# Two matmuls without a use beside each step of the triangular inversion in layer 1

## The chip, the cores and the metric

The kernel runs on one core of a Trainium2 chip. The metric is the device time of one execution in microseconds (us). Before the change it was 2228.44 us, the median of three runs (2225.9 to 2229.92).

A core has five engines, each with a queue of its own that it works through in order: TensorE (PE in the profile; its weight loads are shown apart as PEld), VectorE (DVE), ScalarE (ACT), GpSimd (POOL) and SyncE (SP), which only issues transfers here. An instruction that has to wait for another engine holds up everything behind it in its own queue.

## The reference

Two layers of a transformer trunk over 512 latent tokens and 256 context tokens of width 1024, in fp32. What matters here is the mixer: one input projection feeds a gated DeltaNet in chunks of 64 tokens and a latent attention, side by side. The DeltaNet solves a unit triangular system for every chunk, head and direction.

```python
for l in range(DEPTH):                                   # DEPTH = 2
    h  = modulate(rmsnorm(x, norm1_g[l]), sh1, sc1)
    hc = modulate(rmsnorm(ctx, norm1_g[l]), sh1c, sc1c)
    y, yc = hybrid_mixer(h, hc, ...)                     # input projection, DeltaNet and attention, output projection
    x = x + g1 * y
    x = x + g2 * swiglu(modulate(rmsnorm(x, norm2_g[l]), sh2, sc2), w_gate[l], w_up[l], w_down[l])
    if not last:                                         # the context's own output is only needed in layer 0
        ctx = ctx + g1c * yc
        ctx = ctx + g2c * swiglu(modulate(rmsnorm(ctx, norm2_g[l]), sh2c, sc2c), ...)
return rmsnorm(x, final_norm_g)

# within gdn_chunked, for each chunk of 64 tokens:
a_mat = jnp.where(strict, jnp.einsum('bhnid,bhnjd->bhnij', kb, k) * decay, 0.0)
sol = lax.linalg.triangular_solve(a_mat + eye, rhs, left_side=True, lower=True)
u, w = sol[..., :DV], sol[..., DV:]                      # used by the scan over the chunks
```

## The kernel before

Activations lie with the features on the 128 partitions and the tokens along the row. A matrix product in fp32 is made of three products in fp32r: weights and activations are split into a high and a low part (ScalarE copies the high part, VectorE subtracts it for the low one, `load_w` and `split`), and `gemm` (line 222) issues high x high, high x low and low x high into one PSUM bank. A matmul of line 222 on the latent tokens has a 128 x 128 weight tile and 512 columns.

The program is written as eleven generators, one for each piece of a layer, most of them run once for each layer: the context's input projection, chain, attention and FFN, and the latent stream's `lat_in` (input projection), `lat_chain` (DeltaNet), `mla_prep` and `mla_att` (attention) and `lat_ffn` (output projection and FFN). `weave` runs them by turns, by ranks and paces in the table `TUNE`, and a scheduler behind it settles the order of each engine's queue. Layer 1's context pieces (`ctx_in1`, and `ctx_chain` with l = 1) are woven into layer 0's `lat_ffn`.

`gdn_pre` prepares a group of DeltaNet heads. It is called for the context (CTX, all four head pairs at once) and for the latent stream's head pairs 0 and 1 (X01) and 2 and 3 (X23) one after the other, in each layer: six calls. In the middle of each call the 32 x 32 diagonal blocks are inverted by forward substitution, all blocks side by side:

```python
for r in range(31):
    n, m = 31 - r, r + 1
    t3 = tmp[:, 0:n * m].rearrange("p (a b) -> p a b", b=m)
    tt(t3, L3[:, r + 1:32, r:r + 1].to_broadcast([P, n, m]), M3[:, r:r + 1, 0:m].to_broadcast([P, n, m]))
    tt(M3[:, r + 1:32, 0:m], M3[:, r + 1:32, 0:m], t3, SUB)
    yield 1, 0, 0.5
```

Each step is two VectorE operations (`tt`, recorded at line 140) on up to 256 elements a row. Behind the 31 steps TensorE multiplies the inverted blocks together (lines 586 and 587, then 596 and 597), two multiply-adds on VectorE complete the inverse, and the products of line 621 apply it. `gdn_scan` (its first matmuls at lines 668, 680 and 691) then runs over the chunks.

Other lines that the text names: `together` (233) issues matmuls that share a bank on different parts of the array, among them the modulation of layer 1 (four of 32 x 512 for each tile of weights; its transposition is line 304); `rms_rows` (336) sums squares over the features with a matmul by ones, in fp32, which the hardware runs in pieces; `prep` in the attention finds an upper bound of the scores by matmuls and VectorE's reductions (932 and 933 for latent keys, 937 and 938 for context keys, 945 turns the result); `attend` makes the scores (960), and 977 is the reciprocal of its sums. ScalarE's operations by `act` are at line 152, and VectorE's multiply-add `stt` at 149. PSUM has eight banks, of which the tag "C" has two.

Of the kernel before, what the change touches and what calls it, by code (L numbers as in the profile page):

```python
# [20 lines left out]
P = 128  # L21
# [85 lines left out]
def trunk_kernel(ctx, tc, xin, cc, wmod, small, win, wuq, wuk, wuv, wout, wgu, wdn, cst, rope, out):  # L107
    nc = tc.nc
    V, A, G, PE = nc.vector, nc.scalar, nc.gpsimd, nc.tensor
# [14 lines left out]
    def nm(s):  # L124
        uid[0] += 1
        return f"{s}_{uid[0]}"

    def slot(tag, dt=F32, w=None):
        width = WIDTH[tag]
        t = sp.tile([P, width], dt, name=nm(tag), tag=tag, bufs=BUFS[tag])  # L130
        return t[:, 0:w or width]

    def ps(tag):
        return pp.tile([P, 512], F32, name=nm("ps" + tag), tag=tag, bufs=PSB[tag])
# [4 lines left out]
    def tt(out, a, b, op=ALU.mult, e=None):  # L139
        (e or V).tensor_tensor(out=out, in0=a, in1=b, op=op)  # L140
# [34 lines left out]
    ident_r = cp.tile([P, P], F32R, name="ident_r")  # L175
# [49 lines left out]
    def gemm_f32(w, xs, o):  # L225
        for k, x_ in enumerate(xs):
            PE.matmul(o, w[:, k * P:k * P + P], x_, start=k == 0, stop=k == len(xs) - 1)  # L227

    def together(mms):
        prev = None  # L230
        for mm in mms[::-1]:
            with nullcontext() if prev is None else tc.issue_after(prev.ins):
                prev = mm()  # L233
# [220 lines left out]
    def gdn_pre(l, st, hjs, kf, qf, vf, gt, res):  # L454
# [112 lines left out]
        V.transpose(out=L3, in_=bd.rearrange("p (u i) -> p i u", i=32))  # L567
        M3 = M.rearrange("p (i j) -> p i j", j=32)
        tmp = slot("st", w=256)
        for r in range(31):  # L570
            n, m = 31 - r, r + 1
            t3 = tmp[:, 0:n * m].rearrange("p (a b) -> p a b", b=m)
            tt(t3, L3[:, r + 1:32, r:r + 1].to_broadcast([P, n, m]), M3[:, r:r + 1, 0:m].to_broadcast([P, n, m]))
            tt(M3[:, r + 1:32, 0:m], M3[:, r + 1:32, 0:m], t3, SUB)
            yield 1, 0, 0.5
        x1, x2 = bd, L
        V.transpose(out=x1.rearrange("p (u r) -> p r u", r=32), in_=M3)
# [33 lines left out]
        for dst, lh, rh in ((us, vv, (vs, vs)), (W, ke, vv)):  # L611
            for a in range(0, U, 4):
                pt = ps("B")
                pv = pt.rearrange("p (n d i) -> p n d i", d=2, i=64)
                for q in range(4):
                    n, hi = divmod(a + q, nh)
# [441 lines left out]
    class Mix:  # L1058
# [55 lines left out]
        def stage(self, g):  # L1114
            f = self.f[g]
            if g in self.spilled:
                for kind in "kqv":
                    t = slot("g4")
                    nc.sync.dma_start(out=t.rearrange("p (j t) -> p j t", j=len(g)), in_=f[kind].rearrange("j p t -> p j t"))
                    f[kind] = t  # L1120
            return gdn_pre(self.l, self.st, g, f["k"], f.get("q"), f["v"], self.gates, self.pre[g])
# [329 lines left out]
```

## Time and the profile before

| | |
|---|---|
| median of three runs | 2228.44 us |
| the profiled execution | 2224.78 us |
| its span in the trace | 2223.0 us |
| TensorE busy | 2032.2 us (91%), 16048 matmuls |
| VectorE busy | 1474.6 us (66%), 2904 instructions |
| ScalarE busy | 889.5 us (40%), 1583 instructions |
| mean granted clock of TensorE | 0.946 |

The span is the time from the first to the last instruction that the trace shows of one execution. A busy share is a mean over the whole program and says nothing of a single stage. The granted clock is given as a share of 2.4 GHz: TensorE runs at 2.4 or at 1.2 GHz, and a number between 0.50 and 1.00 is a mixture over the stretch.

### The profile page before, as it was taken

Reading aid. Unit: us, or ns where it says so; the run is one execution under the profiler, and the core shown is the slowest. Engines: PE = TensorE matmul, PEld = TensorE weight load, DVE = VectorE, ACT = ScalarE, POOL = GpSimd, SP = SyncE. Lnnn points to the kernel's source line nnn. Section 1 sums busy time; section 2 is a strip of 40 time slices with the busy share of each in tenths; the row PEclk is TensorE's granted clock in tenths of the full one; section 3 lists DMA queues with packets and bytes.
Section 4 is the critical chain, followed back from the end, with each engine's and each line's share of the span. In section 5 each row is a group of like instructions: output and inputs, shape, how many; then the busy total and the mean of one; then the engine's idle time right before and its main releaser. Section 6 shows DMA issues by size and latency. Waiting matters only on the chain.

```text
span 2223.0 us, 40501 instructions
## 1 busy us (share of the span) xinstructions
PE 2032.2 (91%) x16048; PEld 1591.7 (72%) x16048; DVE 1474.6 (66%) x2904; ACT 889.5 (40%) x1583; POOL 69.6 (3%) x249
## 2 busy tenths in 40 slices
PE   5999988889998899899999998987976989999996
PEld 2876777789995557778888885765644677888885
DVE  4688668876689767769444457887687555444445
ACT  4445365444443534552323234534422234222233
POOL 0000001000000000000000000000000000000000
PEclk8999998899999999999999999996986999999998
DMA  8345514344446202242222236621110022233332
GB/s 327 136 155 188 172 32 124 112 143 132 127 155 208 85 11 80 93 146 91 86 76 96 89 113 221 190 78 29 44 34 11 30 76 76 95 99 96 96 99 76
DMA packets 130638, 240.48 MB, mean 108 GB/s; under 512 B 15185, under 2 KB 30065, under 8 KB 130449
## 3 DMA queue, kind: packets, MB, share of 16 engines
q1 hardware_dynamic: 124592, 224.16, 31.1%
q0 software_dynamic: 5856, 13.74, 2.3%
q8 instruction: 126, 2.06, 0.4%
q14 instruction: 64, 0.52, 0.1%
HBM read 228.30 MB, written 6.91 MB: 106 GB/s over the span
## 4 chain that ended last, share of the span: by engine, by line
PE 76%; DVE 10%; DMA 6%; ACT 5%; issue 3%; SPq 0%; POOL 0%; ACTq 0%; DVEq 0%; POOLq 0%
PE psA L222 35%; PE psM L222 14%; PE psF L222 4%; PE psB L960 3%; PE psA L233 2%; PE psA L227 2%; PE psB L621 2%; PE psM L233 2%; PE psC L668 1%; DVE fl L140 1%; DMA m<-wmod 1%; ACT t L152 1%; DVE g L140 1%; PE psC L680 1%; PE psC L691 1%
## 5 line engine op out<-in xcount | busy, mean ns | idle before, releaser
L222 PE MATMUL psA<-hx,wh 128*128 128x512 f32 x1680 | 537.0, 399 | 24.3 <-ACT hx L152 8.4
L152 ACT ACTIVATE wh<-wr 128x512 fp32r<-128x512 f32 (+2 forms) x410 | 249.1, 608 | 636.4 <-PE psA L222 466.6
L140 DVE TENSOR_TENSOR wl<-wr,wh 128x512 fp32r<-128x512 f32 (+2 forms) x410 | 269.5, 658 | 229.0 <-ACT wh L152 228.4
L222 PEld LDWEIGHTS psA<-hx,wh 128*128 128x128 f32 x1680 | 315.1, 190 | 113.7 <-issue 16.6
L222 PE MATMUL psA<-hx,wl 128*128 128x512 f32 x840 | 330.9, 394 | 1.3 <-DVE wl L140 1.3
L222 PE MATMUL psM<-hx,wh 128*128 128x512 f32 x704 | 217.4, 389 | 0.0
L222 PEld LDWEIGHTS psA<-hx,wl 128*128 128x128 f32 x840 | 159.4, 190 | 36.3 <-DVE wl L140 1.8
L152 ACT ACTIVATE fh<-fr 128x512 fp32r<-128x512 f32 (+3 forms) x186 | 110.7, 599 | 153.8 <-PE psF L222 45.5
L149 DVE SCALAR_TENSOR_TENSOR g<-psA,mod,g 128x512 f32<-128x512 f32 x112 | 83.9, 749 | 104.9 <-PE psA L222 104.6
L222 PEld LDWEIGHTS psM<-hx,wh 128*128 128x128 f32 x704 | 132.2, 188 | 27.2
L140 DVE TENSOR_TENSOR fl<-fr,fh 128x512 fp32r<-128x512 f32 (+3 forms) x186 | 120.0, 648 | 43.3 <-ACT fh L152 39.9
L222 PE MATMUL psM<-hx,wl 128*128 128x512 f32 x352 | 137.0, 389 | 0.0
L222 PE MATMUL psF<-m,fh 128*128 128x256 f32 x600 | 116.3, 292 | 7.1 <-ACT g L152 6.7
L222 PE MATMUL psA<-hd,wh 128*128 128x512 f32 x384 | 120.5, 392 | 0.0
L222 PEld LDWEIGHTS psF<-m,fh 128*128 128x128 f32 x600 | 95.6, 194 | 12.6 <-ACT g L152 9.1
L222 PE MATMUL psA<-ox,wh 128*128 128x512 f32 x320 | 100.7, 393 | 0.0
L222 PE MATMUL psM<-m,fh 128*128 128x256 f32 x416 | 82.1, 295 | 6.9 <-ACT m L152 5.7
L222 PE MATMUL psF<-m,fl 128*128 128x256 f32 x300 | 86.2, 287 | 2.2 <-DVE fl L140 2.1
L222 PEld LDWEIGHTS psA<-hd,wh 128*128 128x128 f32 x384 | 71.7, 188 | 16.4 <-DVE hd L140 1.1
L227 PE MATMUL psA<-m,g 128*128 128x256 f32 x320 | 75.3, 394 | 6.6 <-ACT m L152 3.4
L227 PEld LDWEIGHTS psA<-m,g 128*128 128x128 f32 x320 | 61.8, 197 | 20.3 <-ACT m L152 4.4
L222 PEld LDWEIGHTS psM<-hx,wl 128*128 128x128 f32 x352 | 66.0, 188 | 13.7
(382 smaller groups left out, 3643.0 us busy)
## 6 DMA issues: line engine op xcount, KB each, us to landing
wr<-wgu SPq DMA_DIRECT2D x176, 256.0 KB, 2.6
m<-wmod SPq DMA_DIRECT2D x160, 256.0 KB, 4.0
fr<-wgu SPq DMA_DIRECT2D x88, 256.0 KB, 2.7
wr<-win SPq DMA_DIRECT2D x80, 256.0 KB, 3.3
wr<-wdn SPq DMA_DIRECT2D x64, 256.0 KB, 2.6
g<-win SPq DMA_DIRECT2D x20, 512.0 KB, 6.3
g<-wmod SPq DMA_DIRECT2D x16, 512.0 KB, 10.2
fr<-wdn SPq DMA_DIRECT2D x32, 256.0 KB, 2.7
```

The costliest lines, as they stand in the source:

```text
L140: (e or V).tensor_tensor(out=out, in0=a, in1=b, op=op)
L149: V.scalar_tensor_tensor(out=out, in0=a, scalar=s, in1=b, op0=op0, op1=op1)
L152: A.activation(out, a, f, **kw)
L222: PE.matmul(o, ww[:, wk], xx if n is None else xx[:, a:a + n], start=cnt == 0, stop=cnt == 3 * nk - 1)
L227: PE.matmul(o, w[:, k * P:k * P + P], x_, start=k == 0, stop=k == len(xs) - 1)
L233: prev = mm()
L621: PE.matmul(pv[s, q, d, :], u3(lh[d])[s, c, :], u3(rh[d])[s, c, :], start=True, stop=True)
L668: PE.matmul(o[s], x_[s], y_[s], start=i == 0, stop=i == len(mm) - 1)
L680: PE.matmul(v4(ws)[s, hi, d, :], v4(w)[s, hi, d, :], S[s, hi, d, :], start=True, stop=True)
L691: PE.matmul(v4(kv)[s, hi, d, :], u3(ks[d])[s, unit(hi, n, d), :], v4(u)[s, hi, d, :], start=True, stop=True)
L960: PE.matmul(pst, K[ki][:, b:b + P], Q[qi], start=cnt == 0, stop=cnt == 2)
```

## The change

A new function `spin` issues n matmuls of the identity (128 x 128, fp32r) by itself, repeated four times along the row (512 columns), into a bank of PSUM that nobody reads. `gdn_pre` calls it with n = 2 behind every one of the 31 steps when `l` is 1, whichever the stream. Each added matmul is tied to the VectorE instruction that was written last, by a dependency of the kind NoSync: it sets the order for the scheduler and makes no wait on the chip.

```diff
+    def spin(bank, n):
+        last = next(i for i in reversed(nc.cur_bb.bb.instructions) if i.engine == mybir.EngineType.DVE)
+        for _ in range(n):
+            mm = PE.matmul(bank, ident_r, ident_r.unsqueeze(1).to_broadcast([P, 4, P]), start=True, stop=True)
+            tc.add_manual_dep(mm.ins, last.name, mybir.DependencyInfo(mybir.DependencyClass.NoSync, mybir.DependencyReason.DATA),
+                              reason="spin")
...
         tmp = slot("st", w=256)
+        bank = ps("C") if l else None
         for r in range(31):
             n, m = 31 - r, r + 1
             t3 = tmp[:, 0:n * m].rearrange("p (a b) -> p a b", b=m)
             tt(t3, L3[:, r + 1:32, r:r + 1].to_broadcast([P, n, m]), M3[:, r:r + 1, 0:m].to_broadcast([P, n, m]))
             tt(M3[:, r + 1:32, 0:m], M3[:, r + 1:32, 0:m], t3, SUB)
+            if l:
+                spin(bank, 2)
             yield 1, 0, 0.5
```

Three calls have l = 1, so 186 matmuls are added to the 16048. In the changed kernel the lines behind `gemm_f32` are numbered 7 higher, those from the loop on 8 and behind it 10; line 232 is the added matmul. The queues of TensorE below show where they stand; a row has the line, the operation, the output with the inputs and the size of the result, and x4 means four of them in a row.

The first place is TensorE's queue in layer 0's FFN on the latent tokens, where the context's inversion of layer 1 (the call with CTX and l = 1) is woven in. `ox` and `hd` are the hidden rows, `wh` and `wl` the high and low weights. Before:

```order
L222 MATMUL psA_11102<-ox_10942,wh_11074 128x512
L222 MATMUL psA_11102<-ox_10943,wh_11074 128x512
L222 MATMUL psA_11102<-ox_10942,wl_11075 128x512
L222 MATMUL psA_11126<-hd_10614,wh_11098 128x512
L222 MATMUL psA_11126<-hd_10615,wh_11098 128x512
```

After:

```order
L222 MATMUL psA_11115<-ox_10942,wh_11083 128x512
L222 MATMUL psA_11115<-ox_10943,wh_11083 128x512
L222 MATMUL psA_11115<-ox_10942,wl_11084 128x512
L232 MATMUL psC_11044<-ident_r 128x512 x4
L222 MATMUL psA_11143<-hd_10614,wh_11111 128x512
L222 MATMUL psA_11143<-hd_10615,wh_11111 128x512
```

Four of the added matmuls now stand between two groups of the FFN; in all there are 62 of them in this stretch, in groups of two to six, and the FFN's own matmuls keep their order.

The second place is TensorE's queue at the end of layer 1's input projection, at the start of the products of the first latent call (X01): `hx` are the input rows, `m` and `sc` the modulation, `cst` holds the ones, and `g` are the inverted blocks. Before:

```order
L222 MATMUL psA_15354<-hx_13955,wl_15320 128x512
L233 MATMUL psM_14474<-m_15260,sc 32x512
L233 MATMUL psM_14474<-m_15258,sc 32x512
L233 MATMUL psM_14474<-m_15256,sc 32x512
L233 MATMUL psM_14474<-m_15254,sc 32x512
L304 MATMUL psM_15391<-cst,t_15389 128x8 x4
L336 MATMUL psA_15403<-t_15404,cst 128x512
L586 MATMUL psB_15580<-g_2807_15136,g_2701_14540 32x32
L587 MATMUL psB_15580<-g_2806_15135,g_2702_14541 32x32
```

After:

```order
L240 MATMUL psM_14537<-m_15330,sc 32x512
L232 MATMUL psC_15211<-ident_r 128x512 x4
L311 MATMUL psM_15481<-cst,t_15479 128x8 x4
L232 MATMUL psC_15211<-ident_r 128x512
L343 MATMUL psA_15497<-t_15498,cst 128x512
L232 MATMUL psC_15211<-ident_r 128x512 x28
L343 MATMUL psA_15516<-t_15517,cst 128x512
L343 MATMUL psA_15516<-t_15520,cst 128x512
L232 MATMUL psC_15211<-ident_r 128x512 x3
L596 MATMUL psB_15706<-g_2808_15199,g_2702_14603 32x32
```

Here 31 of the added matmuls stand ahead of the first square sum (line 343, which was 336; 26 of them ahead of the modulation's matmuls), one group of 28 behind it, and 3 behind the next two. The two square sums of the next norm, which stood between the products of lines 586 and 596, now stand ahead of all of them (line 596 is the old 586).

The third place is TensorE's queue in the second latent call (X23), at the maxima of the attention's last preparation: `hx` are queries and keys, `kc` the context's keys. Before:

```order
L932 MATMUL psA_16969<-hx_15452,hx_15474 128x512
L932 MATMUL psA_16972<-hx_15452,hx_15474 128x512
L932 MATMUL psA_16975<-hx_15452,hx_15474 128x512
L937 MATMUL psA_16978<-kc_10491,hx_15474 128x256 x2
L937 MATMUL psA_16982<-kc_10491,hx_15474 128x256 x2
L945 MATMUL psA_16990<-ident_r,mneg_16988 128x128 x4
L233 MATMUL psA_17076<-acc_16788,cst 64x512
```

After:

```order
L942 MATMUL psA_17108<-hx_15546,hx_15568 128x512
L232 MATMUL psC_17026<-ident_r 128x512
L942 MATMUL psA_17111<-hx_15546,hx_15568 128x512
L232 MATMUL psC_17026<-ident_r 128x512 x2
L942 MATMUL psA_17114<-hx_15546,hx_15568 128x512
L232 MATMUL psC_17026<-ident_r 128x512 x2
L947 MATMUL psA_17117<-kc_10491,hx_15568 128x256 x2
L232 MATMUL psC_17026<-ident_r 128x512 x2
L947 MATMUL psA_17121<-kc_10491,hx_15568 128x256 x2
L232 MATMUL psC_17026<-ident_r 128x512 x4
L955 MATMUL psA_17129<-ident_r,mneg_17127 128x128 x4
L232 MATMUL psC_17026<-ident_r 128x512 x5
```

One to five of the added matmuls stand between the maxima's matmuls, and the order of the others is kept.

## Rows read from the trace of the kernel before

**Rows 1.** The page's second part: granted clock in 40 equal slices, in tenths.

```profile
PEclk8999998899999999999999999996986999999998
```

**Rows 2.** Windows view: window, PE, PEld, DVE, ACT, POOL busy (xcount), clock, DMA share, GB/s.

```profile
1060.00:1333.00 273.00, 273.00 (x1846) 223.77 (x1845) 129.40 (x195) 85.03 (x142) 2.19 (x4) 1.00 0.29 91
1467.88:1491.10 23.22, 23.22 (x108) 18.02 (x112) 21.87 (x58) 5.65 (x11) 0.00 (x0) 1.00 0.19 55
1500.46:1514.64 14.18, 8.34 (x265) 4.87 (x265) 7.41 (x11) 9.97 (x15) 0.00 (x0) 0.62 0.01 2
1514.64:1557.40 42.76, 35.05 (x360) 25.73 (x360) 37.69 (x74) 15.52 (x29) 4.71 (x10) 0.70 0.15 40
1645.00:1660.00 15.00, 11.35 (x45) 5.73 (x43) 14.36 (x36) 4.80 (x8) 1.95 (x4) 0.99 0.08 17
1660.00:1702.00 42.00, 23.60 (x60) 12.24 (x58) 35.60 (x82) 8.25 (x15) 0.00 (x0) 0.62 0.06 19
1702.00:1719.40 17.40, 14.28 (x283) 9.40 (x284) 11.72 (x15) 5.15 (x8) 0.00 (x0) 0.55 0.01 2
```

**Rows 3.** VectorE's operations by shape, 1000 to 1060 and 1440 to 1500 us.

```profile
L140 DVE TENSOR_TENSOR st<-g,g 128x256 f32<-128x256 f32 x1 | 0.4, 425 | 0.0
...
L140 DVE TENSOR_TENSOR st<-g,g 128x256 f32<-128x256 f32 x1 | 0.4, 424 | 0.0
```

**Rows 4.** Chain of waits through layer 0's FFN: start, length, what runs (us).

```profile
1028.45 5.44 PE psM L222 x24
...
1218.28 27.40 PE psA L222 x120
```

**Rows 5.** The same chain, 1491 to 1517 us.

```profile
1491.10 1.12 PE psM L233 x8
...
1492.89 1.06 PE psM L304 x8
1493.94 0.96 PE psA L336 x2
1494.90 5.56 issue
...
1503.84 4.12 PE psA L336 x4
...
1514.64 2.39 PE psB L621 x38
```

**Rows 6.** Timeline of PE and DVE: start, length, instruction, wait before it.

```profile
1648.74 0.40 PE L932 MATMUL psA<-hx,hx 128*128 128x512 f32 x1
...
1692.83 0.79 PE L932 MATMUL psA<-hd,hd 128*128 128x512 f32 x1 [1.20 <-DVE mx L933]
...
1695.38 0.69 DVE L933 TENSOR_REDUCE mx<-psA 128x1 f32<-128x512 f32 x1 [0.28 <-PE psA L932]
```

**Rows 7.** DVE's waits, 1660 to 1702: us in total, times, longest us.

```profile
DVE acc L140 <- PE psA L233: 1.5, 1, 1.5
DVE hx L140 <- PE psA L222: 1.1, 1, 1.1
DVE mx L933 <- PE psA L932: 1.0, 4, 0.3
DVE mx L938 <- PE psA L937: 1.0, 3, 0.4
DVE t L977 <- PE psA L233: 0.8, 1, 0.8
```

**Rows 8.** The same view, 1702 to 1719.4.

```profile
DVE mx L933 <- PE psA L932: 3.0, 3, 1.2
DVE mx L938 <- PE psA L937: 1.9, 2, 1.0
```

**Rows 9.** Chain of waits, 1714 to 1720: first and last of four.

```profile
1714.78 1.58 PE psB L960 x3
...
1718.47 0.89 PE psB L960 x3
```

## The prediction

> **What bounds the kernel now.** I read the slices of the page first. The row of granted clocks [rows 1] stands at 8 tenths or more everywhere but in two of its 40 slices, the 28th and the 31st, which fall to 6. A slice is 55.6 us long, so they lie between 1500 and 1723 us, and that is layer 1's mixer. So I cut the program into stages with the windows view [rows 2]; a clock of 1.00 there is 2.4 GHz, 0.50 is 1.2 GHz. What to see is which engine has no idle time. From 1060 to 1333 us (layer 0's latent FFN) TensorE is busy 273.00 of 273.00 us at clock 1.00, VectorE 129.40: TensorE alone is the limit. From 1467.88 to 1491.10 (the last four column chunks of layer 1's input projection) TensorE is full again, and VectorE nearly is (21.87 of 23.22). From 1660 to 1702 it is the other way round: VectorE 35.60 of 42.00, TensorE 23.60 at a mean clock of 0.62, so about three quarters of that time at 1.2 GHz. From 1702 to 1719.4 TensorE is busy 14.28 of 17.40 at 0.55.
>
> Then I looked for the triangular inversions, by the VectorE operations by shape [rows 3]: the step with 256 elements stands once in each inversion. The first answer shows that between 1000 and 1060 us there is an inversion as well. That is the context stage of layer 1: it has l = 1, and the new code asks only for `l`, not for the latent stream. So three stages get 62 matmuls each, 186 in all, and one of them lies in the FFN of layer 0, where TensorE is full at full clock.
>
> **The change part by part.** One added matmul has 128 partitions by 512 columns in fp32r, as those of line 222 have. In the chain through the FFN [rows 4] 24 of those take 5.44 us, 0.227 each, and 120 take 27.40, 0.228. No trace of before has a matmul whose result nobody reads, so its price is bounded from both sides: below by the modulation's eight in 1.12 us, 0.14 each (they use only 32 columns of the array), above by the square-sum's pieces, two in 0.96, 0.48 each [rows 5]. I take 0.227: same line form, type and shape. The order shows that no added matmul waits for VectorE; they run as soon as TensorE's queue reaches them.
>
> (The Trainium skill, "TensorE: Matmul & The Clock Gate", section "Back-to-back issue gap", gives about 131 ns for a sustained matmul of 512 columns in a real stream. By it the 62 of the context stage would cost an estimated 8.1 us. The row shows 227 ns in such a stream, and the row decides.)
>
> *Context stage.* 62 x 0.227 = +14.1 us. They stand inside a stream without idle time; nothing covers them and nothing is gained, since the clock is already 1.00. If TensorE had slack there, they would be free, but 273.00 of 273.00 leaves none.
>
> *First latent stage.* 26 added matmuls stand within the last four column chunks and the modulation's matmuls, 36 behind them. On VectorE the weight splits stand further back among the inversion's steps than before, so the steps themselves need not wait. TensorE: the last chunk ended at 1491.10 [rows 5]; with 22 added ahead of it that is 1491.1 + 22 x 0.227 = 1496.1. Then 8 added (1.8) and the eight modulation matmuls (1.12) give 1499.0; the turn of the modulation, one more and the first square sum (1.06 + 0.23 + 0.96) give 1501.3; 28 added (6.4) give 1507.6; the two square sums of the query norm now stand here, four pieces of 0.48, done at 1509.5. Before, the same sums took 4.12 us at half clock behind the stage's first products and ended at 1503.84 + 4.12 = 1507.96. So the norm's chain is 1.5 us later. The 28 fill the wait of 5.56 us that stood there, and some more. What is late next: the stage's products can start only at 1510, not 1500.46, and in VectorE's queue the two multiply-adds before the next matmuls (line 621, 1514.64 before) now stand behind about six more row operations of some 0.7 us. Line 621 may thus start 6 us later; but those operations are then done, and VectorE has 42.76 - 37.69 = 5.07 us of idle time up to 1557.4 [rows 2] to take up the rest. I take +2.0; the bounds are 1.5 - 5.1 = -3.6 (all that idle time vanishes with the clock) and +6.
>
> *Second latent stage.* Here the clock is half, and here is the gain. One 128x512 matmul takes 0.40 at full clock and 0.79 at half [rows 6]. VectorE's waits for TensorE between 1660 and 1702 [rows 7] add up to 1.5 + 1.1 + 1.0 + 1.0 + 0.8 = 5.4 us. The seven waits for maxima (2.0) are at most 0.4 each, no more than a full-clock matmul gives back: all 2.0 go. The 1.5 for the accumulator's reader goes nearly (1.3). Before the other two (1.9) four and five added matmuls stand in the queue, some 1 us each, so half is kept: 0.9. Sum -4.2. Between 1702 and 1719.4 five waits for maxima take 3.0 + 1.9 [rows 8], and 0.39 less each is -1.9; then the four pieces of TensorE work from 1714.78 to 1719.37 [rows 9], 4.6 us partly at half clock, would take about 3.2, -1.4. Against this, 12 added matmuls stand between 1645 and 1660, where TensorE is busy 11.35 of 15.00 and VectorE 14.36: 2.7 us, mostly in TensorE's gaps; I charge +0.5. In all -7.0. The bounds: all 5.4 and 4.9 and 1.4 give -11.7; a clock that falls all the same and 12 matmuls on the path give +2.7. I take a value nearer the gain because the added matmuls fill just the waits between the maxima: two take 0.45 at full clock, and VectorE's reduction, during which TensorE waited, takes 0.69 [rows 6].
>
> After 1719.4 TensorE is the limit at full clock; what is gained there is passed on. PSUM has two buffers for the tag of the added bank; the stage's scan takes the other one, and its readers are long done, so I cost that at nothing.
>
> **Sum.** 14.1 + 2.0 - 7.0 = +9.1 us. The profiled execution took 2224.78 us, so 2233.9; the median of the runs is 3.7 above it, so **2237**. Its own range is 2233 to 2243. About 0.2% (4.5 us) is what a measurement of this kernel can tell from no change.
>
> **The rivals.**
> - *The warm clock returns more.* All of VectorE's waits in the second stage go (-11.7) and the first stage gains (-3 instead of +2): 14.1 - 3 - 11.7 = -0.6, 2228: no change. For it: the half clock also stretches what ACT waits for. Against: some added matmuls stand before the very reads that VectorE waits for. Chance 0.17.
> - *TensorE is the limit wherever its clock is half* (the other side). The time at half clock is (1 - clock) / 0.5 of each window: of the busy times in [rows 2] 0.76 x 8.34 + 0.60 x 35.05 + 0.76 x 23.60 + 0.90 x 14.28 = 58 us. If all of this halved, 29 us would go: 14.1 + 1.5 - 29 = -13, 2224. It decides from a gain of 18.6 on. Against: VectorE has no such idle time (5.1 + 6.4 + 5.7 in the three later windows), and from 1515 to 1557 no matmul is added. Chance 0.06.
> - *The clock falls all the same.* The added matmuls don't wait for the step they are written beside; 28 of 62 run in one burst, and where TensorE then waits for VectorE it idles as before. With the gain of the second stage down to 1 and the first at +3: 14.1 + 3 - 1 = +16, 2244. For it: in the stretch behind the second inversion nothing is added. Against: there the matmuls come in twos between waits. Chance 0.17.
> - *An added matmul is cheap.* With the same weights each time and a result that nobody adds to, it might run at the modulation's 0.14: 62 x 0.14 = 8.7, and 8.7 + 2 - 7 = +3.7, 2232: within 0.2%. The Trainium skill's 131 ns of the sentence above would give the same sign and size. Against: every 128x512 matmul of line 222 has its own weight load and keeps to 0.227. Chance 0.06.
> - The forecast: 0.54.
>
> Slower by over 0.2%: 0.54 + 0.17 = 0.71. Within: 0.17 + 0.06 = 0.23. Faster: 0.06. The range for 8 in 10 takes in the first rival and the third: 2226 to 2246.
>
> **What would show it.** In the profile after, the end of layer 0's FFN should be 14 us later, with 62 matmuls of the new line between about 1000 and 1080 us, 0.227 apart, at clock 1.00. In the first latent stage 28 of them should stand in one burst after the input projection, and line 621 should start some 20 us later than before (14 + 6). In the second, the windows between the 15th and the last step should show a clock near 1.00 instead of 0.62, and the reductions' waits for TensorE should be near nothing. I am wrong if the FFN is not longer by the matmuls' number times their pace, or if the time from the second inversion's start to the FFN of layer 1 shrinks by more than 12 us.

## The result and the profile after

The changed kernel takes 2253.26 us (median of 4 runs, 2252.55 to 2257.07) against 2229.18 us for the kernel before (the three runs of the first table and one more): the ratio is 1.0112, with a 95% interval of 1.0097 to 1.0127. That is 24 to 25 us slower. Slower was forecast, but by 9 us, and the range ended at 2246.

The head of the page after, its row of granted clocks, and the windows that answer to [rows 2] (columns as there):

```profile
span 2250.7 us, 40874 instructions
...
PE 2079.4 (92%) x16234; PEld 1630.8 (72%) x16234; DVE 1476.1 (66%) x2904; ACT 890.1 (40%) x1583; POOL 69.7 (3%) x249
...
PEclk8999988899999999999999999998988999999998
```

```profile
1011.00:1106.00 95.00, 93.59 (x653) 76.43 (x652) 60.99 (x120) 25.23 (x41) 0.00 (x0) 1.00 0.26 78
1106.00:1340.00 234.00, 234.00 (x1433) 192.21 (x1432) 108.87 (x163) 70.30 (x117) 0.00 (x0) 1.00 0.28 88
1486.00:1534.10 48.10, 46.40 (x204) 33.83 (x203) 37.23 (x87) 17.46 (x27) 0.00 (x0) 0.96 0.13 41
1534.10:1590.00 55.90, 43.13 (x651) 31.58 (x649) 42.40 (x82) 23.35 (x41) 4.54 (x10) 0.79 0.12 33
1688.00:1731.00 43.00, 34.02 (x119) 19.20 (x118) 38.10 (x86) 9.68 (x17) 0.00 (x0) 0.88 0.06 19
1731.00:1747.10 16.10, 13.00 (x290) 8.43 (x291) 11.01 (x15) 4.77 (x8) 0.00 (x0) 0.68 0.01 3
```

The clock did rise: no slice is at 6 any more, and the second latent stage has 0.88 and 0.68 where it had 0.62 and 0.55. It did not pay.

To see where the time went, I matched every TensorE instruction of the trace after with the same one before and took the difference of their starts. Its median is read in quiet windows (by before's time 985 to 1000, 1090 to 1110, 1455 to 1466, 1580 to 1600, 1634 to 1644, 1725 to 1745 and 2190 to 2215 us), and what it grows by from one to the next belongs to the stage between. An example: the first product behind the inversion of the first latent stage begins at 1494.90 + 5.56 = 1500.46 before [rows 5] and at 1534.6 after, so it is 34.2 us late there.

| growth of the lag, us | context stage | first latent stage | scan behind it | second latent stage | rest | sum |
|---|---|---|---|---|---|---|
| forecast | +14.1 | +2.0 | 0 | -7.0 | 0 | +9.1 |
| changed kernel | +16.5 | +7.4 | +1.3 | -2.2 | +0.3 | +22.9 |

(The sum, of unrounded figures, has the -0.3 between the first two as well.) How far the lag can be trusted shows in stages that a kernel leaves as they were: there it grows by 0.5 or less in most of the runs below, and by 1.0 at most; only the scan and the rest jump by up to 1.6 either way. Ahead of the first added matmul, where the programs are the same, thirteen traces lag 3.0 to 11.2 us behind before's (4.8 for this one). That is scatter from run to run, it limits what medians tell to some 3 us, and so the stages are compared by the lag and only the whole by medians. The thirteen lags have a mean of 6.7, and the median of before stands some 4 above its own profiled execution; whether the other 3 are more than scatter stays open. Each ratio below is taken against runs of the kernel before made beside it (medians 2227.07 to 2229.15 us).

**Context stage.** The chain of waits after shows the added matmuls one by one on the path:

```profile
1016.28 1.39 PE psC L232 x6
1017.90 0.46 PE psC L232 x2
1018.82 0.93 PE psC L232 x4
1022.50 0.94 PE psC L232 x4
```

Four take 0.93 to 0.94, up to 0.235 each, where 0.227 was taken.

**First latent stage.** The chain of waits after, from the end of the inversion (lines 587 and 588 are its transposes) to line 631, the old 621:

```profile
1516.82 0.52 DVE g L587
...
1518.71 2.05 DVE g L588
...
1520.79 0.72 ACT g L152
1521.51 0.49 ACT t L152
...
1522.04 1.06 PE psM L311 x8
...
1523.43 1.33 PE psA L343 x2
1524.76 7.55 PE psC L232 x28
1532.31 1.73 PE psA L343 x4
...
1540.98 1.22 PE psA L222 x2
...
1542.57 4.56 PE psA L222 x10
...
1549.85 3.84 PE psB L631 x82
```

ScalarE's copy of the modulation's rows (`t` at 1521.51) stands behind `g` at 1520.79, which had to wait for VectorE's transposes. In the kernel before, ScalarE's timeline has that copy ahead of them, and the first `g` comes 6 us behind it:

```profile
1492.24 0.60 ACT L152 ACTIVATE t<-psM 128x512 f32<-128x512 f32 x1 [0.43 <-PE psM L233]
...
1496.34 0.63 ACT L152 ACTIVATE t<-t 128x512 f32<-128x512 f32 x1 [1.68 <-DVE t L146]
1498.60 0.72 ACT L152 ACTIVATE g<-g,cst 128x512 f32<-128x512 f32 x1 [1.63 <-DVE g L577]
```

What hangs on the copy are the modulation's transposition, the sums of squares and two norms in which ScalarE, VectorE and TensorE take turns. Before, the first of the two ran beside the inversion's last steps and its transposes. After, both come when the inversion is over, one behind the other, and the stage's products wait for both. Twelve matmuls of line 222 (1.22 + 4.56 us), which stood behind line 621's first products before, now stand ahead of line 631 as well.

**Second latent stage.** VectorE's waits from 1688 to 1747.1, which answer to [rows 7, 8]:

```profile
DVE mx L943 <- PE psA L942: 3.0, 5, 0.9
DVE mx L948 <- PE psA L947: 2.8, 4, 1.0
DVE acc L140 <- PE psA L240: 2.4, 1, 2.4
DVE acc L140 <- ACT t L152: 0.6, 1, 0.6
```

The reader of the accumulator waits longer than before (2.4, was 1.5), and the maxima still wait 5.8 in all. Up to 1732 us, about the inversion's last step, they wait 1.5 of it; the other 4.3 lie behind:

```profile
DVE mx L948 <- PE psA L947: 0.8, 2, 0.4
DVE mx L943 <- PE psA L942: 0.7, 2, 0.3
```

TensorE's timeline shows why the accumulator's reader waits: the sum (line 240) stands behind two added matmuls, which take 0.98 us there, 0.49 each, so at half clock:

```profile
1712.40 1.05 PE L232 MATMUL psC<-ident_r 128*128 128x512 f32 x2
1713.38 1.78 PE L240 MATMUL psA<-acc,m 128*64 128x512 f32 x4
```

### The profile page after: what moved, and what is told of

Its sections match the earlier page's. It is cut to its first block, busy times and chain, and to the rows that moved or that the text cites. A ratio compares the mean times of both kernels' runs of the same rounds, so it can differ in the third digit from the quotient of the medians.

```text
span 2250.7 us, 40874 instructions
## 1 busy us (share of the span) xinstructions
PE 2079.4 (92%) x16234; PEld 1630.8 (72%) x16234; DVE 1476.1 (66%) x2904; ACT 890.1 (40%) x1583; POOL 69.7 (3%) x249
## 4 chain that ended last, share of the span: by engine, by line
PE 74%; DVE 13%; DMA 6%; ACT 4%; issue 3%; SPq 0%; POOL 0%; ACTq 0%; DVEq 0%; POOLq 0%
PE psA L222 34%; PE psM L222 13%; PE psF L222 4%; PE psB L970 3%; PE psA L227 2%; PE psA L240 2%; PE psB L631 2%; DVE g L140 2%; DVE fl L140 2%; PE psM L240 1%; PE psC L678 1%; PE psC L232 1%; PE psC L690 1%; DMA m<-wmod 1%; ACT t L152 1%
```

## The experiments

The theory that the profile after suggests: the matmuls' own time costs what was forecast, and the rest is the new order of ScalarE's and VectorE's queues, which the scheduler chose because TensorE's queue was fuller. The rival: the added matmuls' time alone makes all of it. In four kernels only the choice of the stage or the number differs:

```diff
-        bank = ps("C") if l else None
+        bank = ps("C") if l and st is CTX else None                    # context alone
+        bank = ps("C") if l and st is LAT and hjs[0] == 0 else None    # first latent call alone
+        bank = ps("C") if l and st is LAT and hjs[0] == 2 else None    # second latent call alone
...
-                spin(bank, 2)
+                spin(bank, 1)                                          # second call, one a step
```

**Context alone.**

> The added matmuls stand in the context's call alone (62 of 186). By the prediction's step they cost 62 x 0.227 = 14.1 us, so about 14 over the kernel before. By the offsets between the two traces this stage took 15 to 16. If the 5 us by which the changed kernel's trace already lags behind before its first added matmul belong to the change (a rival), this kernel shows them too, in the trace up to 1000 us, and its time is some 20 over.

Measured 2244.09 us, ratio 1.007 (1.0048 to 1.0092). The stage's lag grows by 15.5.

**First latent call alone.**

> The added matmuls stand in the first latent call alone. The prediction's step says +2.0 us (bounds -3.6 to +6). By the offsets between the two traces it is about +8: if that is the stage's own cost and not one that the later start brings, this kernel is 7 to 9 us slower.

Measured 2236.31 us, ratio 1.0047 (1.0032 to 1.0062); the stage +6.9. So the cost is the stage's own, and not one that a later start brings.

**Second latent call alone.**

> The added matmuls stand in the second latent call alone. The prediction's step says -7.0 us (bounds -11.7 to +2.7). By the offsets between the two traces it is -1 to -2, so a time that can hardly be told from the kernel before. Up to 1645 us the program is that of the kernel before, so the trace up to there also shows how much two executions of the same program differ: with the 5 us lag as mere scatter, 0 to 8.

Measured 2224.46 us, ratio 0.9991 (0.9976 to 1.0007): no change that can be told. The stage -3.6.

**One a step in the second call.**

> The second latent call alone, with one matmul beside each step instead of two. If the gain there is limited by VectorE's own work (35.6 of 42 us busy before) and two are more than the clock needs, one gives the same -3 us or a bit more, since the accumulator's reader waits for fewer of them (2.4 us with two, 1.5 before). If the clock needs two, it falls as before and the gain is gone: 0.

Measured 2229.99 us, ratio 1.0015 (0.9995 to 1.0034). The stage is 3.6 us *longer*, with the clock at 0.61 over the same steps:

```profile
1672.00:1734.00 62.00, 46.92 (x362) 25.94 (x361) 47.66 (x95) 13.40 (x23) 0.00 (x0) 0.61 0.05 14
```

Neither theory had that. One matmul a step did not hold the clock; what the 3.6 are made of, the matmuls or this kernel's own new order, no run here separates.

**Narrow matmuls in the changed kernel's order.** The instructions are cut once every queue is settled:

```diff
+    def cut(a):
+        ap = [list(a.ap[0]), [1, 32]]
...
+    for b in nc.cur_f.blocks:
+        ins = list(b.instructions)
+        for k, i in enumerate(ins):
+            if i.name in SPINS:
+                ins[k] = type(i)(name=i.name, ins=[cut(i.ins[0]), i.ins[1]], outs=[cut(i.outs[0])],
...
```

> The changed kernel with its 186 added matmuls cut to 32 columns after the order is settled, so that every queue keeps the changed kernel's order word for word. If the cost is the matmuls' own time on TensorE, little is left of it: the context stage takes at most 62 x 0.06 = 4 us more, the first latent stage near nothing, and the clock falls in the second as before; together 0 to +6. If a good part is the new order of VectorE's queue (weight splits behind steps of the inversion), the first latent stage still loses 4 us or more, and the whole is +6 to +12.

Measured 2251.75 us, ratio 1.0112 (1.0096 to 1.0129), as slow as the changed kernel. Context +10.4, first stage +8.2, second +2.0. With the matmuls a sixteenth as wide, the first latent stage lost as much as in the changed kernel, so in this order their length was not its cost.

**The order alone.** The added matmuls that neither signal anything nor wait for anything are taken out of the settled queue; 13 of the 186 stay, none in the context's stage, 3 in the first latent stage and 10 in the second.

```diff
+    for b in nc.cur_f.blocks:
+        b.instructions = [i for i in b.instructions if i.name not in SPINS or i.has_update() or i.has_wait()]
```

> The order of the changed kernel in all queues, with the added matmuls taken out of TensorE's queue after the order is settled (a few that signal a semaphore stay). New theory: the first latent stage's cost is the order and nothing else. Before, ScalarE copied the modulation's rows and the two norms' chains ran beside the inversion; now that copy stands behind ScalarE's first copies of the inverted blocks, and both norms run ahead of the stage's products. Then the stage still loses 7 to 8.5 us here, the context stage 2 to 3 (its waits for weight splits with the narrow matmuls were 2.4), and the second latent stage nothing: together +9 to +12. If the cost is the matmuls' time on TensorE (the prediction's way), the kernel is back at the time before, within 3.

Measured 2245.93 us, ratio 1.0077 (1.006 to 1.0094). Without its matmuls the change still costs 17 us: context +6.4, first latent stage +9.3, second 0.0. The first stage's figure is the theory's. There the copy of the modulation's rows holds up TensorE, as ScalarE's timeline and then TensorE's show:

```profile
1508.86 0.72 ACT L155 ACTIVATE g<-g,cst 128x512 f32<-128x512 f32 x1 [9.18 <-DVE g L591]
...
1511.32 0.58 ACT L155 ACTIVATE t<-psM 128x512 f32<-128x512 f32 x1
```

```profile
1503.06 1.07 PE L244 MATMUL psM<-m,sc 128*32 128x512 f32 x8
1511.95 1.88 PE L315 MATMUL psM<-cst,t 128*128 128x8 f32 x8 [7.82 <-ACT t L155]
```

The modulation's matmuls begin at 1503.06, but the copy waits behind `g` until 1511.32, and TensorE waits 7.82 us for it. In the kernel before, the copy began 1.14 us after those matmuls did (1491.10 [rows 5] and 1492.24). How much of the 9.3 this copy alone makes is not shown, since VectorE's and TensorE's queues have their new order too.

The context's cost is twice the 2 to 3 expected. There TensorE is idle for 5.0 us (busy 79.96 of the 85.00 from 1011 to 1096; before, 80.00 of the 80.00 from 1005 to 1085), and its weight loads wait for the splits of the weights:

```profile
PEld psA L225 <- ACT wh L155: 3.8, 3, 1.6
PEld psM L225 <- DVE wl L143: 2.4, 1, 2.4
```

Weight loads overlap matmuls (65.83 us of them ran in those 80.00), so these waits are not the cost itself.

**The added matmuls alone.** The counterpart: the kernel before, all queues as they were, and the 186 put into TensorE's settled queue at the changed kernel's places. `FILL` says ahead of which matmul, counted from the start, how many are put.

```diff
+FILL = {5908: 6, 5909: 2, 5911: 4, 5923: 4,
...
+        8329: 4, 8333: 1, 8334: 28, 8336: 3,
...
+        9289: 4, 9293: 2}
```

> The counterpart of the run with the order alone: all 186 added matmuls at the changed kernel's places in TensorE's queue, and the order of everything else as before. By the prediction's arithmetic: context +14.1 (at the 0.235 us that the trace shows for one, 14.6), first latent stage +2 (28 in a burst of 6.6 us stand in a wait of 5.56), second -7. If the order is what made the difference, the context is 14 to 15, the first stage at most +2, and the second -2 to -4, since VectorE's waits behind the inversion stay; in all +11 to +14, against +24 with the order changed.

Measured 2251.98 us, ratio 1.0112 (1.0098 to 1.0126). Context +15.5, first stage +5.1, second 0.0: +20.8 by the lag. Both theories missed here. The order is not all of the first stage's cost: the matmuls alone cost 5.1, the order alone 9.3, and the two together 7.4, less than the sum, because the matmuls fill waits that the order opens. Of the 5.1, all is there before the inversion's products begin: at the end of the input projection the lag has grown by 5.2, the price of the 22 matmuls that stand in its last chunks (22 x 0.235 = 5.2), where TensorE was busy 23.22 of 23.22 us [rows 2]. What comes behind it, the burst of 28 in the wait included, ends by costing nothing. In the second stage the first maxima (1670 to 1690 us) now wait 2.7 and 0.3 for TensorE, where the same reductions had waited 0.3 in all, and that eats the gain that follows:

```profile
DVE mx L936 <- PE psA L935: 2.7, 2, 1.9
DVE mx L941 <- PE psA L940: 0.3, 1, 0.3
```

**Twenty behind the last step.** Only the first latent call, only at the end:

```diff
+            if bank is not None and r == 30:
+                spin(bank, 20)
```

> Only the first latent call, and only behind its last step: 20 added matmuls, 4.7 us of TensorE's time in the wait of 5.56 us that stood there, with the order of ScalarE and VectorE nearly that of before. If the cost of the first latent stage is the order, this has none of it, and the clock, which falls at 1496 us before, stays up longer: the square sum that took 4.12 us at half clock takes about 2, and the stage is 0 to 3 us shorter. If added matmuls there cost their own time, it is 3 to 5 us longer.

Measured 2234.4 us, ratio 1.0026 (1.001 to 1.0042); the stage +4.0. The twenty stand in the wait, but the scheduler again put the second norm's square sums ahead of a part of the products.

**The same twenty and the second call.** The edit above and two a step in the second call.

> Two matmuls beside each step of the second latent call, and the 20 behind the last step of the first; none in the context's call. With -3.3 for the second (the stage alone measured that) and 0 to -3 for the first: -3 to -6 against the kernel before, the fastest so far. If the 20 cost their own time, it is +1.

Measured 2231.17 us, ratio 1.0009 (0.9996 to 1.0023); first stage +4.2, second -3.7. The two add up, and cancel.

**Twenty into the wait, with no queue changed.** As in the run of the matmuls alone, but only ahead of the stage's first product (place 8334: 20). 

> The kernel before, with every queue's order as it was, and 20 added matmuls put into TensorE's queue right ahead of the first latent stage's products, where it waited 5.56 us. 20 x 0.235 = 4.7 us fit in that wait. If the first stage's cost was the order, they cost nothing here, and the stage gains what the clock gives back: the square sum of 4.12 us halves, but VectorE and ScalarE's chain remains, so 0 to -3. With the order changed a little, the same 20 cost 4.0. If added matmuls cost their time even in a wait, it is +4 here too.

Measured 2231.44 us, ratio 1.0018 (1.0004 to 1.0032); the stage -0.5. Its trace lags by 9.2 us ahead of the change and by 9.24 at the end, so in the profiled execution nothing of the ratio comes from the added matmuls; that the medians' 4 us come from ahead of the change, as the 9.2 do, is likely but not shown. By the lag, twenty matmuls in a wait cost nothing when no queue is reordered, and 4.0 when one is. They also gained next to nothing.

**All of the latent stages' waits filled.** No queue reordered, nothing in the context's stage:

```diff
+FILL = {8334: 20, 8398: 4, 8464: 12, 8466: 2, 8621: 7, 8624: 2, 8625: 3, 8626: 4,
+        9230: 2, 9232: 6, 9236: 2, 9240: 1, 9241: 3, 9242: 3, 9243: 3, 9245: 3, 9247: 6, 9251: 2, 9274: 14,
+        9281: 10, 9282: 4, 9283: 3, 9284: 3, 9285: 3, 9287: 3, 9289: 5, 9293: 2, 9294: 7, 9361: 1}
```

> The order of before, nothing in the context's stage, and added matmuls only where TensorE waits in the two latent stages, as many as fit into each wait (54 in the first, 83 in the second, up to 20 at one place). If the clock is worth what the half-clock waits show, the first stage gains 1 to 4 us and the second 4 to 7 (the waits for maxima behind the inversion's steps too): -5 to -10, the fastest version. If VectorE is the limit throughout, it gains no more than the second stage alone did, -3.6.

Measured 2221.0 us, ratio 0.997 (0.9956 to 0.9984): faster than both kernels, as expected. (The second stage has 86 of them, not 83.) First stage -1.0, second -8.5, the rest +1.6. The windows view over the second stage, of the kernel before, of this one, and of the next:

```profile
1660.00:1719.40 59.40, 37.88 (x341) 21.64 (x341) 47.31 (x96) 13.40 (x23) 0.00 (x0) 0.60 0.04 14
```

```profile
1668.60:1719.60 51.00, 43.63 (x421) 26.74 (x421) 46.50 (x96) 13.55 (x24) 0.00 (x0) 1.00 0.05 17
```

```profile
1661.60:1721.00 59.40, 48.76 (x415) 36.44 (x413) 47.32 (x96) 13.41 (x23) 0.00 (x0) 0.60 0.04 14
```

VectorE's 96 operations stretch over 59.40 us in the first and 51.00 in the second, and VectorE's waits for TensorE in that stretch fall from 10.3 to 3.3:

```profile
DVE mx L936 <- PE psA L935: 1.8, 3, 0.6
DVE mx L941 <- PE psA L940: 1.2, 2, 0.6
DVE hx L143 <- PE psA L225: 0.3, 1, 0.3
```

In the first latent stage the clock rises too, from 0.62 and 0.70 [rows 2, third and fourth window] to 0.88 and 0.85, but only 1.0 us comes back. The same two stretches, with this run's lag:

```profile
1509.90:1524.00 14.10, 11.25 (x282) 6.99 (x282) 7.36 (x11) 9.84 (x15) 0.00 (x0) 0.88 0.01 2
1524.00:1565.50 41.50, 35.78 (x379) 26.21 (x379) 37.50 (x75) 15.95 (x30) 4.72 (x10) 0.85 0.17 44
```

**The same with 32 columns.** Same places, same number:

```diff
-                    bank = mk(o, [[512, 128], [1, 512]], o.bass_ap.tensor)
-                    x = mk(src, [[128, 128], [0, 4], [1, 128]], src.bass_ap.tensor)
+                    bank = mk(o, [[512, 128], [1, 32]], o.bass_ap.tensor)
+                    x = mk(src, [[128, 128], [1, 32]], src.bass_ap.tensor)
```

> The same added matmuls as in the run that fills the waits, at the same places and with the same number, but with 32 columns instead of 512. If the 8.5 us that the second latent stage gained there come from TensorE's clock and the clock from the work in the waits, the clock falls again as before (about 55 us at half between the 15th step and the end of the inversion's products) and the stage is within 1.5 us of the kernel before. If it is enough that something is issued in the waits, it gains 8 again.

Measured 2228.68 us, ratio 1.0 (0.9986 to 1.0014); second stage +0.1. The third window above is this kernel's: the clock is 0.60, as before. So the second stage's 8.5 us come from the clock, and the clock from what the wide matmuls did in the waits; something issued there is not enough.

## Why the prediction was wrong, point by point

*That the context's call is in it, and costs.* Right in mechanism. The matmul's price is 0.235, not 0.227, with 62 x 0.235 = 14.6. The stage cost 15.5 with the order kept, 15.5 with the context's call alone and the order changed, and 16.5 in the changed kernel, against 14.1; the last 1.0 is no more than such a stage moves unaided. The Trainium skill's 131 ns for such a matmul ("TensorE: Matmul & The Clock Gate", "Back-to-back issue gap") does not hold here: the row shows 235. With that the rival of the cheap matmul falls.

*The first latent stage, +2.0.* This is the step that failed: "Line 621 may thus start 6 us later", of which VectorE's "5.07 us of idle time" were to take up 4. In the changed kernel the lag is 20.9 us at the stage's start and 34.9 at that line (now 631), so it starts 14.0 later. Of these 6.6 came back, more than the 4 that I counted on, and +7.4 stayed. Three things were wrong in it.

The first shows with the order kept: there line 621 starts 6.0 us later (its lag of 27.2, less the 21.1 at the stage's start), but only 0.9 came back, and the stage is +5.1. That 6.0 is the number forecast is luck, since I had worked it out from the new order, which this run does not have. What I had at 1496.1 instead of 1491.1 were 22 matmuls in a stream without idle time; I charged such matmuls at their full price in the context's stage, and here let VectorE's idle time pay for them.

The second is that I read the new order on TensorE and VectorE alone. On ScalarE the modulation's copy had moved behind the first copies of the inverted blocks, and with it both norms behind the inversion. The new order of all queues costs +9.3 without the added matmuls. In the changed kernel the copy is 8.2 us later (1521.41 - 1492.24 - 20.94), about 6 of them because the modulation's matmuls stand behind 26 added ones, the other 2 because of `g`. I saw that "the two square sums of the query norm now stand here" and put the norm's chain at 1.5 us later; its sums end 5.1 later (1534.04 - 1507.96 - 20.94).

The third is that twelve matmuls of line 222 (5.8 us) now stand ahead of line 631, which my sum does not have. They are work brought forward, and so part of what came back later. In the changed kernel line 631 starts 1549.85 - 1514.64 = 35.2 us later, 30.4 without the 4.8 from ahead of the change, and not "some 20".

*The second latent stage, -7.0.* The clock rose as forecast up to the inversion's last step, though to 0.88 and not "near 1.00". Up to there the lag fell by 2.5 us, where 3.7 was forecast (4.2 less the 0.5 charged): of the waits of 5.4 us [rows 7] 2.4 + 0.8 + 0.7 = 3.9 stay from 1688 to 1732, where 1.2 were to stay. The one that I had vanish to 0.2, the accumulator's, grew to 2.4, with two added matmuls ahead of its sum. Behind the inversion the forecast 1.9 + 1.4 us were not returned, and 0.3 was lost: nothing is added there, and the clock was mostly at half again (0.68). The third rival named that stretch; I gave it 0.17 and counted the gain in the forecast all the same. With the waits filled, behind the inversion too, the stage does gain 8.5, within the bound of 11.7.

*The sum.* 14.1 + 2.0 - 7.0 = 9.1 became 16.5 + 7.4 - 2.2 = 21.7, and 1.3 + 0.3 - 0.3 in stretches that jump by as much unaided. In the trace, 4.8 us of lag from ahead of the change come on top. The rival of the falling clock, at +16, comes nearest in its number, but its mechanism, a clock that falls where nothing is added, explains at most the 3.6 us missed behind the second inversion. Of the rest, 5.4 are the first stage's, 2.4 the context's, and 1.2 the waits before the second inversion's end.

*The rival of the other side* (29 us if TensorE's half clock were the limit everywhere) is refuted. By it the second stage alone had (0.76 x 23.60 + 0.90 x 14.28) / 2 = 15.4 us to give; at a full clock in that whole stage 8.5 came back, and VectorE is busy 46.50 of 51.00 us. In the first stage the clock rose to 0.88 and 0.85 and 1.0 came back. Its time was also put down wrongly: 2228 - 13 is 2215, and 2224 is only where it begins to decide.

What stays open: why the scheduler orders the norms as it does for 20 matmuls in an idle wait, how much of the new order's 9.3 us ScalarE's copy makes by itself, and how much more the first latent stage could give, where the filled waits brought only 1.0 us.

## What to carry to other kernels

Matmuls that keep TensorE's clock up paid here only where they fit into waits: 62 in a full stream cost 15.5 us, and 86 in the waits of one stage gained 8.5. A higher clock alone says little: it gave back 8.5 us in one stage here and 1.0 in the other. Under a scheduler an added instruction is also a change of order on engines that never run it; run the new order without the added work, and the added work in the old order, before believing in either. Read the order on every engine that shares a chain with the changed stretch: here ScalarE's, which I had not looked at, kept TensorE waiting 7.82 us in the run with the order alone.

## What the runs showed of the hardware

With 86 matmuls of 512 columns in the second latent stage's waits the granted clock there was 1.00; with the same 86 at 32 columns it was 0.60, and with one matmul a step 0.61. And a narrow matmul is not free in a full stream: in the context's call the 62 with 32 columns, in the changed order, added 10.4 - 6.4 = 4.0 us to the order alone, where the wide ones added 16.5 - 6.4 = 10.1: 0.4 of the time for a sixteenth of the columns. The rows agree: six narrow ones in a row take 0.58 us (1018.34 to 1018.92 in that run's trace), six wide ones 1.39.
